# Two heads side by side in the scratch of branch outputs, and the first raw left operands loaded ahead of the last key panel

## The chip, the core and the metric

The kernel runs on one core of a Trainium2 chip. The metric is device time in microseconds. The engines are named as in the profile: PE (matrix products; PEld its weight loads), DVE (elementwise work, scans, 32x32 transposes), ACT (activations, copies; it also issues DMAs), POOL (masks, and DMAs), SP (issues DMAs only). Each engine runs its own queue in order.

## The reference

One inference step of a layer with 16 heads on 1024 prompt rows (one stream) and 128 sample rows (8 streams of 16): an input projection, eight stick-breaking heads, eight retention heads with a rotary embedding, per-head normalisation and gate, one output projection, a residual.

```python
def merge(o_sb, o_r, gate_sb, gate_r, g_sb, g_r, w_out):
    y_sb = head_rms_norm(o_sb, g_sb, gate_sb.dtype) * jax.nn.silu(gate_sb)
    y_r = head_rms_norm(o_r, g_r, gate_r.dtype) * jax.nn.silu(gate_r)
    y = jnp.concatenate([y_sb, y_r], axis=-1)
    return jnp.einsum('bte,ed->btd', y, w_out)
...
    log_beta = jax.nn.log_sigmoid(z)
    log_keep = jnp.where(strict, jax.nn.log_sigmoid(-z), 0.0)
    later = lax.cumsum(log_keep, axis=3, reverse=True) - log_keep
    a = jnp.where(strict, jnp.exp(log_beta + later), 0.0)
    return jnp.einsum('bhqk,bkhd->bqhd', a.astype(v.dtype), v)
...
    scores = jnp.einsum('bihd,bjhd->bhij', qf, kf) * intra[None]
    o = jnp.einsum('bhij,bjhe->bihe', scores, vf)
    o = o + jnp.einsum('bihd,bhde->bihe', qf, sf) * decay_read.T[None, :, :, None]
    s_new = sf * jnp.exp(lg * jnp.float32(n))[None, :, :, None] + jnp.einsum('bjhd,hj,bjhe->bhde', kf, decay_write, vf)
```

All results are float32. Each product of two float32 operands is made as three matmuls: both operands are split into a high and a low part (`wh` and `wl` for weights, `mh` and `ml` or `ah` and `al` for the other side; ACT makes the high part, DVE the low one), and high x high, high x low and low x high are added.

## The kernel before

**Stages.** Rows are worked in two groups: group 0 is row tiles 0 to 3 and the sample rows, group 1 is row tiles 4 to 7. Phase 0 does the eight heads for group 0, phase 1 for group 1. For each head of phase 1 the panels are, in order: `rows` (value and gate rows), `ret_keys` and `ret_queries` (the rotary key and query `rk` and `rq`), `attention` (stick-breaking). For the last head the order is `rows, attention, ret_keys, ret_last`: `ret_last` makes the last query panel. A panel (`project`) takes four weight loads `wr<-w_cols` (L389), each split into `wh` and `wl`, and 48 matmuls `acc` (L400).

**The output product** comes last, from about 1867 us. It is made by seven block products in Strassen's manner, numbered 1 to 7 (`n` below), each in two halves. Their left operands are branch outputs or sums of branch outputs, their right ones blocks of `w_out` or sums of them (`s_b`). A product loads its right operand in eight blocks `wr` (L1227, five buffers that it shares with the panels), splits each (L170, L171), and makes three matmuls a block and row tile (L1210, L1213, L1214). The first six halves, `FIRST`, begin while the last heads' attention and retention still finish between them.

**The scratch in between.** A finished branch output of one head (128 x rows of the group) is stored to `s_y`, one DRAM tensor a head; sums of its quarters (`sum_rows`, run by the generator `sums`, tile `br`) are stored to `s_s`, one tensor a head. `left` (L339) fetches the raw left operand of one product from there: eight heads in tiles `mr` or `yr` of two heads each, three tiles deep for `mr`, and one load a head. It issues the first three tiles, waits `wait` steps (`D_LEFT` = 18 for group 0), and then splits one head at a step into `mh` and `ml`; every second split lets the next tile be loaded. `left_sample` (L356) does the same for sample rows.

**The order of the work.** It is written by the program, not by the chip: `tick()` is called after each matmul of a panel and several times a block of a product, and each tick lets one due `Job` (a generator) emit its next step; the number it yields is how many ticks later the next step is due. `drain(job)` ticks until that job is done. `pin` holds an instruction at its place among the matmuls.

**Retention keys.** `ret_branch` needs the keys with rows and columns exchanged. It stores `rk` to `s_rk` (L648), waits `D_TO`, reads it back in four pieces into `ro` (L657: on POOL in phase 0, on SP in phase 1), waits `D_RK` (36 ticks in phase 0, 22 in phase 1), and then transposes on DVE into `rkn` (L1035), scales it (L1039), and goes on to scores `rs` (L913), outputs `pa` (L931, L936) and the state `pS` (L946). Stick-breaking weights go the same way: masks on POOL (L682), scan on DVE (L693), product `be` (L694), store `s_be` (L648), read-back (L657), transpose to `kp` (L753), and the matmuls `pa` (L790).

**The first left operand.** The product that opens the output stage, number 5 of group 0, needs its left operand `mr<-s_s` during `ret_last`: `first_left` drains the sums (`summed[0]`), and calls `left`; the panel `ret_last` is then made with its splits between the matmuls. `early_sums` are the sums of group 1's rows.

Of the kernel before, what the change touches and what calls it, by code (L numbers as in the profile page):

```python
# [21 lines left out]
H = 8  # L22
# [25 lines left out]
D_TB = (17, 24)  # L48
D_TI = (36, 13)
D_LATE = 8  # L50
D_RK = (36, 22)
D_OUT = 3
V_SET = 4
D_SUM = 6
# [4 lines left out]
D_FIN = 2  # L59
D_MR = 6  # L60
D_OP = 2
D_LEFT = 18
D_SUM2 = (4, 6, 26)
D_SUM3 = (3, 3, 6)
MR = 3
# [26 lines left out]
def tile_hybrid_step(  # L92
# [44 lines left out]
    def y_rows(t):  # L137
# [21 lines left out]
    s_v = [scr.tile([P, 4, P], F32, name=f"s_v{h}") for h in range(H)]  # L159
    s_S = [scr.tile([P, P], F32, name=f"s_S{h}") for h in range(H)]  # L160
    s_b = [[scr.tile([P, 4, 512], F32, name=f"s_b{n}_{k}") for k in range(HT)] for n in range(2)]
    s_s = [[scr.tile([P, 4, 256], F32, name=f"s_s{i}_{h}") for h in range(H)] for i in range(2)]
    s_y = [
        [scr.tile([P, g["n"]], F32, name=f"s_y{i}_{e}") for e in range(2 * H)]
        for i, g in enumerate(GROUPS)
    ]

    def split(hi, lo, src):
        return (
# [87 lines left out]
    def drain(job):  # L257
        while job is not None and not job.done:
            tick()
# [40 lines left out]
    def sum_rows(gi, h):  # L300
        def load(r):
            for kk in range(2):
                pin(nc.sync.dma_start(r[:, 2 * kk : 2 * kk + 2].rearrange("p a n -> p (a n)"), s_y[gi][kk * H + h][:, :512]))

        ops = ((3, 1, 3, "a"), (1, 0, 1, "s"), (0, 3, 0, "s"), (2, 2, 0, "s"))
        return load, ops, s_s[gi][h]

    def sums(pool, items, pace, bufs):

        def fetch(load):  # L310
            r = pool.tile([P, 4, 256], F32, name="br", tag="br", bufs=bufs)
            load(r)
            return r

        r = fetch(items[0][0])
        yield pace[2]
        for i, (_, ops, dst) in enumerate(items):
            nxt = fetch(items[i + 1][0]) if i + 1 < len(items) else None
            for o, a, b, how in ops:
                pin(nc.vector.tensor_tensor(r[:, o], r[:, a], r[:, b], ALU.add if how == "a" else ALU.subtract))  # L320
                yield pace[0]
            yield pace[1]
            pin(nc.scalar.dma_start(dst, r))
            r = nxt
            yield pace[2]

    def left(gi, n, hi, lo, bufs, tag, deep, wait):
        src = LEFT[n]
        raw = []

        def load(pair):
            r = bufs.tile([P, 2, 256], F32, name=tag, tag=tag, bufs=deep)
            for i in range(2):
                h = 2 * pair + i
                if src[0] == "y":
                    rows = s_y[gi][src[1] * H + h][:, src[2] * 256 : src[2] * 256 + 256]
                else:
                    rows = s_s[gi][h][:, src[1], :]
                pin(nc.sync.dma_start(r[:, i], rows))  # L339
                raw.append(r[:, i])  # L340

        for pair in range(deep):
            load(pair)
        yield wait
        for h in range(HT):
            pin(*split(hi[h], lo[h], raw.pop(0)))
            if h % 2 and h // 2 + deep < HT // 2:
                load(h // 2 + deep)
            yield D_OP

    def left_sample(kk, hi, lo, bufs, tag, deep, wait):
        raw = []
        for part in range(2):
            r = bufs.tile([P, HT // 2, P], F32, name=tag, tag=tag, bufs=deep)
            for i in range(HT // 2):
                pin(nc.sync.dma_start(r[:, i], s_y[0][kk * H + part * HT // 2 + i][:, 4 * P : 5 * P]))  # L356
                raw.append(r[:, i])
# [113 lines left out]
    with ExitStack() as s1:  # L471
# [332 lines left out]
        def decode(h, qs, rest):  # L804
# [99 lines left out]
                )  # L904
            out.done(0)
            oT = op.tile([P, P], F32, name="doT", tag="doT", bufs=1)
            Job(out.finish(0, 0, h, 4, oT, s_y[0][h][:, 4 * P : 5 * P]))

        def retention(gi, g, h, out, rq, rk, rkn, rv, dT):
            def scores(i, kind):  # L910
# [111 lines left out]
        def ret_branch(gi, g, h, rows_in, rk):  # L1022
            rv = values[gi, h][:, :, 1, :]
            nt = len(g["tiles"])
            rkn = ep.tile([P, 6, P], F32, name="rkn", tag="rkn")

            out = Out(nt, "ro")
            dT = op.tile([P, 2, P], F32, name="dT", tag="dT", bufs=1)
            tied(nc.sync.dma_start(dT, c_dt[:, h]))
            s = turn_out(rk[:, : nt * P].rearrange("p (k t) -> p k t", t=P), f"s_rk{gi}_{h}")  # L1030
            yield D_TO[phase[0]]
            raw = out.o.rearrange("p k d -> p (k d)")
            turn_in(s, raw, back[phase[0]])
            yield D_RK[phase[0]]
            tied(nc.vector.transpose(rkn.rearrange("p k d -> p (k d)")[:, : nt * P], raw))  # L1035
# [3 lines left out]
            nc.vector.tensor_scalar(rkn[:, :4, :], rkn[:, :4, :], dec[:, h, 1:2], None, ALU.mult)  # L1039
# [3 lines left out]
            yield from out.finish(1, gi, h, 0, rkn.rearrange("p k d -> p (k d)"), s_y[gi][H + h])  # L1043

        def sb_branch(gi, g, h, out, q2, k2, kT, rest):
            tiles, nt = g["tiles"], len(g["tiles"])
            off = 0 if gi == 0 else 4
            nc.scalar.dma_start(k_prompt[h, :, tiles[0] * P : (tiles[0] + 4) * P], kT[:, :NB_TOK])
            if SAMPLE in tiles:
                nc.scalar.dma_start(k_sample[h], kT[:, 4 * P : 5 * P])  # L1050
            if gi == 0:
                nc.scalar.dma_start(s_k[h], kT[:, :NB_TOK])
            yield D_NAT[phase[0]]
            rows = yield from stick_breaking(g, h, out, q2, k2, rest)
            store_rows(tiles, values[gi, h][:, :, 0, :], v_prompt, v_sample, h)
            if gi == 0:
                nc.scalar.dma_start(s_v[h], values[gi, h][:, :4, 0, :])
            yield from out.finish(0, gi, h, 0, rows[2][1] if gi else kT, s_y[gi][h][:, :NB_TOK])
# [5 lines left out]
        summed, sampled, mine = [], [], {}  # L1064

        def kept(i):
            return [[half[i][:, h // 2, h % 2 * 256 : h % 2 * 256 + 256] for h in range(HT)] for half in mov]
# [8 lines left out]
            return left_sample(0, *mine["s", 0], wp, "mr", MR, D_LEFT)  # L1076

        def first_left():
            drain(summed[0])
            mine[0, 5] = kept(0)  # L1080
            return left(0, 5, *mine[0, 5], wp, "mr", MR, D_LEFT)

# [2 lines left out]
        for gi, g in enumerate(GROUPS):  # L1085
# [6 lines left out]
            for h in range(H):  # L1092
# [11 lines left out]
                def ret_queries(acc=None):  # L1104
                    rows_in["rq"] = rope(acc or project(g, mov, col(4, h)), "rq", *ropes)

                def ret_keys(acc=None):
                    nonlocal ret_job
                    acc = acc or project(g, mov, col(5, h))
                    drain(ret_job)  # L1110
                    ret_job = Job(ret_branch(gi, g, h, rows_in, rope(acc, "rk", *ropes)), D_NAT[phase[0]])

                def ret_last():
                    rest = first_left()
                    next(rest)
                    ret_queries(project(g, mov, col(4, h), rest))
                    for _ in rest:
                        pass
                    drain(sampled[0])

# [177 lines left out]
    with ExitStack() as s3:  # L1298
# [112 lines left out]
        ready = [Job(left_sample(1, *mine["s", 1], fp, "ys", 2, D_LEFT // 2), 24)]  # L1411
# [195 lines left out]
```

## Time and profile before

| | |
|---|---|
| median of three runs | 2256.67 us (2253.02, 2256.67, 2259.68) |
| profiled execution | 2256.29 us |
| its span in the profile | 2254.4 us |
| mean granted clock of PE | 0.996 |
| phase 1, end of the last panel | about 1867 us after the start |
| first products (`FIRST`) | about 1867 to 1979 us |
| DMA traffic | 471.24 MB, 209 GB/s on average |

A row of the timeline gives the start, the time from the first to the last of the instructions it joins, engine, line of the kernel, operation, what is written and read, and how many; brackets hold the engine's idle time before it and what ended it. SPq rows are DMAs that SP issues: the time is that of issuing, not of the transfer. A row of the waits tells what PE stood still for: total, number of times, longest. A row of windows gives the busy time of PE, PEld, DVE, ACT and POOL, then PE's granted clock, the busy share of the 16 DMA engines and GB/s. A 128x512 matmul is listed with 0.39 us but one starts every 0.23 us, since they overlap.

### The profile page before, as it was taken

How to read it: one execution, taken by the hardware profiler on the slowest of the kernel's cores; microseconds unless marked ns; L12 is line 12 of the kernel's file. 1: busy time of each engine (PE TensorE's matmuls, PEld its weight loads, DVE VectorE, ACT ScalarE, POOL GpSimd, SP SyncE). 2: the span in 40 equal slices, each digit the busy share in tenths (PEclk: the TensorE clock that was granted, in tenths of full speed). 3: DMA queues.
4: the chain of work that ended last, by engine and by line, in shares of the span. 5: the costliest groups of instructions: out<-in, count | busy, mean ns of one | idle time of the engine just before them, and what ended most of it. 6: DMA issues, size and time to landing. Idle time of an engine off the chain costs nothing.

```text
span 2254.4 us, 34741 instructions
## 1 busy us (share of the span) xinstructions
PE 2219.5 (98%) x12002; PEld 1884.7 (84%) x12002; DVE 1266.5 (56%) x2688; ACT 922.2 (41%) x2000; POOL 434.6 (19%) x724
## 2 busy tenths in 40 slices
PE   8999999999999999999999999999999999999998
PEld 7888889798888979888788888888888887778886
DVE  5335445453554545355666665766566666556677
ACT  6423333333333333334434344343433445545563
POOL 1022131322213232221312112020302212000020
PEclk9999999999999999999999999999999999999999
DMA  8567575576656657577768887887888776865786
GB/s 295 168 198 201 176 198 176 174 195 205 190 178 188 195 173 200 186 206 266 234 187 228 241 232 236 243 229 231 232 238 230 226 210 182 226 217 162 218 217 175
DMA packets 383984, 471.24 MB, mean 209 GB/s; under 512 B 121408, under 2 KB 238656, under 8 KB 383296
## 3 DMA queue, kind: packets, MB, share of 16 engines
q1 hardware_dynamic: 253712, 290.98, 43.7%
q0 software_dynamic: 36432, 95.72, 15.2%
q10 hardware_dynamic: 93664, 82.33, 11.9%
q8 instruction: 94, 1.54, 0.3%
q14 instruction: 82, 0.67, 0.1%
HBM read 367.97 MB, written 110.36 MB: 212 GB/s over the span
## 4 chain that ended last, share of the span: by engine, by line
PE 86%; DMA 6%; DVE 3%; issue 3%; ACT 1%; POOL 0%; SPq 0%; ACTq 0%; DVEq 0%; POOLq 0%
PE accm L457 33%; PE acc L400 28%; PE a L1214 5%; PE a L1213 5%; PE a L1210 5%; PE z L763 2%; PE pa L790 2%; PE zc L831 1%; DMA wr<-w_out 1%; PE pd L892 1%; DMA xc<-x_cols 1%; PE rs L913 1%; PE pa L931 1%; PE pS L946 1%; DMA wr<-w_cols 1%
## 5 line engine op out<-in xcount | busy, mean ns | idle before, releaser
L170 ACT ACTIVATE wh<-wr 128x512 fp32r<-128x512 f32 x408 | 257.1, 631 | 486.6 <-PE acc L400 207.2
L457 PE MATMUL accm<-whn,mh 128*128 128x512 f32 x1152 | 452.6, 393 | 2.0 <-DVE rq L503 1.0
L457 PE MATMUL accm<-whn,ml 128*128 128x512 f32 x1152 | 451.9, 393 | 0.0
L457 PE MATMUL accm<-wln,mh 128*128 128x512 f32 x1152 | 451.5, 392 | 0.0
L400 PE MATMUL acc<-mh,wh 128*128 128x256 f32 (+2 forms) x1536 | 444.0, 340 | 7.5 <-ACT wh L170 7.5
L400 PE MATMUL acc<-ml,wh 128*128 128x256 f32 (+2 forms) x1536 | 445.0, 340 | 0.0
L400 PE MATMUL acc<-mh,wl 128*128 128x256 f32 (+2 forms) x1536 | 443.5, 339 | 0.0
L171 DVE TENSOR_TENSOR wl<-wr,wh 128x512 fp32r<-128x512 f32 x408 | 279.6, 688 | 281.8 <-ACT wh L170 258.2
L171 DVE TENSOR_TENSOR wln<-wrn,whn 128x512 fp32r<-128x512 f32 x256 | 175.3, 688 | 270.7 <-ACT whn L170 268.0
L170 ACT ACTIVATE whn<-wrn 128x512 fp32r<-128x512 f32 x256 | 161.2, 632 | 393.4 <-PE accm L457 258.8
L400 PEld LDWEIGHTS acc<-mh,wh 128*128 128x128 f32 x1536 | 283.8, 189 | 26.7 <-ACT wh L170 7.5
L400 PEld LDWEIGHTS acc<-mh,wl 128*128 128x128 f32 x1536 | 281.7, 188 | 24.4 <-issue 5.4
L400 PEld LDWEIGHTS acc<-ml,wh 128*128 128x128 f32 x1536 | 281.1, 189 | 19.1 <-issue 1.2
L457 PEld LDWEIGHTS accm<-whn,mh 128*128 128x128 f32 x1152 | 216.5, 188 | 47.5 <-DVE rq L503 2.1
L457 PEld LDWEIGHTS accm<-whn,ml 128*128 128x128 f32 x1152 | 216.5, 188 | 43.5 <-issue 0.8
L457 PEld LDWEIGHTS accm<-wln,mh 128*128 128x128 f32 x1152 | 216.4, 188 | 42.9
L657 POOL DMA_DIRECT2D be<-s_be x128 | 93.8, 739 | 160.6 <-DMA s_be<-be 132.9
L693 DVE TENSOR_TENSOR_SCAN kp<-kp 128x1152 f32<-128x1152 f32 (+4 forms) x40 | 82.6, 2066 | 64.5 <-POOL kp L682 36.5
L1210 PE MATMUL a<-wh,mh 128*128 128x512 f32 x240 | 95.6, 398 | 0.8 <-ACT mh L1270 0.8
L1213 PE MATMUL a<-wl,mh 128*128 128x512 f32 x240 | 94.4, 393 | 1.5 <-DVE wl L171 1.4
L1214 PE MATMUL a<-wh,ml 128*128 128x512 f32 x240 | 94.4, 393 | 0.0
L682 POOL TENSOR_SCALAR_AFFINE_SELECT kp<-kp 128x128 f32<-128x128 f32 x40 | 13.7, 342 | 374.3 <-ACT kp L676 369.2
(287 smaller groups left out, 3002.7 us busy)
## 6 DMA issues: line engine op xcount, KB each, us to landing
wr<-w_cols SPq DMA_DIRECT2D x256, 256.0 KB, 4.5
wrn<-w_rows SPq DMA_DIRECT2D x256, 256.0 KB, 3.7
kcT<-cache_k POOLq DMA_DIRECT2D x64, 512.0 KB, 5.0
vc<-cache_v SPq DMA_DIRECT2D x64, 512.0 KB, 5.4
wr<-s_b SPq DMA_DIRECT2D x80, 256.0 KB, 4.2
wr<-w_out SPq DMA_DIRECT2D x80, 256.0 KB, 4.2
br<-w_out SPq DMA_DIRECT2D x64, 256.0 KB, 4.8
s_b<-br ACTq DMA_DIRECT2D x32, 512.0 KB, 5.2
```

Source lines behind the costliest of these rows:

```text
L170: nc.scalar.activation(hi, src, AF.Copy),
L171: nc.vector.tensor_tensor(lo, src, hi.bitcast(F32), ALU.subtract),
L400: last = nc.tensor.matmul(a[:, :m], lhs[:, j, :], rhs[w][:, j, o : o + m], start=(w == 0 and j == 0 and n == 0), stop=(w == KT // WQ - 1 a ...
L457: anchor[0] = nc.tensor.matmul(banks[t], lhs[q][:, j, ts], rhs, start=(k == 0 and n == 0), stop=(k == KT - 1 and n == 2),)
L657: q.dma_start(raw[32 * i : 32 * i + 32, :].rearrange("p (k a) -> p k a", a=32), s[:, :, 32 * i : 32 * i + 32].rearrange("k (j b) a -> b (k ...
L693: nc.vector.tensor_tensor_scan(rev, rev, rev, 1.0, ALU.mult, ALU.bypass)
L763: nc.tensor.matmul(z[:, :c], q2[a][:, i * P : (i + 1) * P], k2[b][:, s : s + c], start=(m == 0), stop=(m == 2),)
L790: nc.tensor.matmul(po[:, :P], at[:, j, :], rest["vn"][j], start=(j == 0), stop=(j == t))
L831: mm = nc.tensor.matmul(z[r, :], qp[:, j, r], ks[2 * j + c // 2][0][:, c % 2, :], start=(j == 0), stop=(j == 1),)
L1210: ins = nc.tensor.matmul(a, hi[k][:, ts], wh, start=first, stop=False)
L1213: nc.tensor.matmul(a, hi[k][:, ts], wl, start=False, stop=False)
L1214: anchor[0] = nc.tensor.matmul(a, lo[k][:, ts], wh, start=False, stop=last)
```

## The change

Scratch tensors `s_s` and `s_y` now hold two heads side by side (`y_of` gives one head's part). `left` fetches a tile of two heads in one load of 128x2x256 instead of two of 128x256, and `left_sample` makes four loads of 128x2x128 instead of eight. `first_left` is called at the start of the last head's `ret_keys`, one panel earlier, so that its first three loads are issued there; it no longer drains the sums whole, but ticks until the sums of group 0's rows are stored (`stored`); `ret_last` drains the rest. `D_RK` grows from 22 to 28 ticks in phase 1, `D_LEFT` from 18 to 24; the last stage's wait goes from `D_LEFT // 2` = 9 to `D_LEFT // 3` = 8. What is computed stays.

```diff
-D_RK = (36, 22)
+D_RK = (36, 28)
-D_LEFT = 18
+D_LEFT = 24
-    s_s = [[scr.tile([P, 4, 256], F32, name=f"s_s{i}_{h}") for h in range(H)] for i in range(2)]
+    s_s = [[scr.tile([P, 2, 4, 256], F32, name=f"s_s{i}_{p}") for p in range(H // 2)] for i in range(2)]
     s_y = [
-        [scr.tile([P, g["n"]], F32, name=f"s_y{i}_{e}") for e in range(2 * H)]
+        [scr.tile([P, 2, g["n"]], F32, name=f"s_y{i}_{p}") for p in range(H)]
...
+    def y_of(gi, e):
+        return s_y[gi][e // 2][:, e % 2, :]
...
+            stored[0] += 1
...
             r = bufs.tile([P, 2, 256], F32, name=tag, tag=tag, bufs=deep)
-            for i in range(2):
-                h = 2 * pair + i
-                if src[0] == "y":
-                    rows = s_y[gi][src[1] * H + h][:, src[2] * 256 : src[2] * 256 + 256]
-                else:
-                    rows = s_s[gi][h][:, src[1], :]
-                pin(nc.sync.dma_start(r[:, i], rows))
-                raw.append(r[:, i])
+            if src[0] == "y":
+                rows = s_y[gi][src[1] * H // 2 + pair][:, :, src[2] * 256 : src[2] * 256 + 256]
+            else:
+                rows = s_s[gi][pair][:, :, src[1], :]
+            pin(nc.sync.dma_start(r, rows))
+            raw.extend((r[:, 0], r[:, 1]))
...
         def first_left():
-            drain(summed[0])
+            while stored[0] < HT + H:
+                tick()
...
                 def ret_keys(acc=None):
                     nonlocal ret_job
+                    if (gi, h) == (1, H - 1):
+                        lefts.append(first_left())
+                        next(lefts[0])
...
                 def ret_last():
-                    rest = first_left()
-                    next(rest)
-                    ret_queries(project(g, mov, col(4, h), rest))
-                    for _ in rest:
+                    drain(summed[0])
+                    ret_queries(project(g, mov, col(4, h), lefts[0]))
+                    for _ in lefts[0]:
                         pass
...
-                made.append(left(g, n, *mine[g, n], *((rp, "yr", 2) if g else (wp, "mr", MR)), D_LEFT // 2))
+                made.append(left(g, n, *mine[g, n], *((rp, "yr", 2) if g else (wp, "mr", MR)), D_LEFT // 3))
```

The order of instructions is the same through phase 0; from the middle of phase 1 it differs. Three places:

SP's queue at the end of the last head, before (`so` is the read-back of attention rows, `br` the sums of group 1, `wr<-w_cols` the last key panel, `wr<-s_b` the first product, `mr` its raw left operand, `ro<-s_rk` the key read-back):

```order
L657 DMA so<-s_o_6_4_1_18140 32x16x32 x4
L303 DMA br<-s_y_13_167 128x512
L389 DMA wr<-w_cols 128x512
L1227 DMA wr_18526<-s_b_0_106 128x512
L1227 DMA wr_18532<-s_b_1_107 128x512
L1227 DMA wr_18538<-s_b_2_108 128x512
L1227 DMA wr_18587<-s_b_3_109 128x512
L339 DMA mr<-s_s_0_122 128x256
L339 DMA mr<-s_s_1_123 128x256
L339 DMA mr<-s_s_2_124 128x256
L339 DMA mr<-s_s_3_125 128x256
L339 DMA mr<-s_s_4_126 128x256
```

The same queue with the change:

```order
L662 DMA so<-s_o_6_4_1_18113 32x16x32 x4
L343 DMA mr<-s_s_0_122 128x2x256
L343 DMA mr<-s_s_1_123 128x2x256
L343 DMA mr<-s_s_2_124 128x2x256
L306 DMA br<-s_y_2_140 128x512
L306 DMA br<-s_y_6_144 128x512
L394 DMA wr<-w_cols 128x512 x2
L1235 DMA wr_18494<-s_b_0_106 128x512
L1235 DMA wr_18500<-s_b_1_107 128x512
L1235 DMA wr_18506<-s_b_2_108 128x512
L1235 DMA wr_18547<-s_b_3_109 128x512
L1235 DMA wr_18570<-s_b_4_110 128x512
```

Three double loads stand ahead of the first four blocks of `s_b`, where six single ones stood behind them; the fourth pair now follows `s_b_4`, and two loads of the key panel and two of `br` come behind the three.

POOL's queue for the last head's attention weights, before (`s_be_6` and `s_be_7` are its last two row tiles):

```order
L648 DMA s_be_6_18659<-be 128x7x128
L657 DMA be<-s_be_6_18659 32x28x32 x4
L682 AFFINE_SELECT kp<-kp 128x128
L682 AFFINE_SELECT be<-be 128x128
L648 DMA s_be_7_18801<-be 128x8x128
```

With the change:

```order
L653 DMA s_be_6_18626<-be 128x7x128
L687 AFFINE_SELECT kp<-kp 128x128
L687 AFFINE_SELECT be<-be 128x128
L662 DMA be<-s_be_6_18626 32x28x32 x4
L653 DMA s_be_7_18785<-be 128x8x128
```

The masks of the last row tile come ahead of the read-back of the one before. On DVE, the scan of that tile before:

```order
L719 SCALAR_TENSOR_TENSOR ro<-ro,or,gg 128x128 x4
L171 TENSOR_TENSOR wl_18789<-wr_18786,wh_18788 128x512
L171 TENSOR_TENSOR wl_18818<-wr_18815,wh_18817 128x512
L793 COPY so<-pa 128x128
L171 TENSOR_TENSOR wl_18856<-wr_18853,wh_18855 128x512
L171 TENSOR_TENSOR wl_18876<-wr_18873,wh_18875 128x512
L693 SCALAR_TENSOR_TENSOR kp<-kp 128x1024
```

With the change (the block `wl_18757` is what `wl_18789` was):

```order
L956 SCALAR_TENSOR_TENSOR S<-S,pS 128x128
L698 SCALAR_TENSOR_TENSOR kp<-kp 128x1024
L945 SCALAR_TENSOR_TENSOR ro<-pa,dec,ro 128x128
L699 TENSOR_TENSOR be<-be,kp 128x1024
L956 SCALAR_TENSOR_TENSOR S<-S,pS 128x128
L190 TENSOR_SCALAR ov<-ssq_18372 128x4
L174 TENSOR_TENSOR wl_18757<-wr_18754,wh_18756 128x512
```

The scan and the product `be` have moved ahead of the norm (`ov`, then `ro`) and of four weight splits.

SP's queue at the key read-back of retention head 4 in phase 1, before (`br<-w_out` feeds the sums of weights):

```order
L657 DMA ro<-s_rk_4_15237 32x16x32
L295 DMA br<-w_out 128x2x256 x2
L657 DMA ro<-s_rk_4_15237 32x16x32 x3
L389 DMA wr<-w_cols 128x512 x2
L448 DMA wrn<-w_rows 128x512
```

With the change:

```order
L394 DMA wr<-w_cols 128x512 x3
L662 DMA ro<-s_rk_4_15213 32x16x32 x4
L298 DMA br<-w_out 128x2x256 x2
L394 DMA wr<-w_cols 128x512 x2
L453 DMA wrn<-w_rows 128x512
```

The four pieces of the read-back are no longer parted by two loads for the sums, which now follow them.

More of the change, by code (lines that the diff above doesn't have):

```diff
@@ L302, in load @@
             for kk in range(2):
-                pin(nc.sync.dma_start(r[:, 2 * kk : 2 * kk + 2].rearrange("p a n -> p (a n)"), s_y[gi][kk * H + h][:, :512]))
+                pin(nc.sync.dma_start(r[:, 2 * kk : 2 * kk + 2].rearrange("p a n -> p (a n)"), y_of(gi, kk * H + h)[:, :512]))
         ops = ((3, 1, 3, "a"), (1, 0, 1, "s"), (0, 3, 0, "s"), (2, 2, 0, "s"))
-        return load, ops, s_s[gi][h]
+        return load, ops, s_s[gi][h // 2][:, h % 2]
+    stored = [0]
     def sums(pool, items, pace, bufs):
@@ L354, in left_sample @@
             r = bufs.tile([P, HT // 2, P], F32, name=tag, tag=tag, bufs=deep)
-            for i in range(HT // 2):
-                pin(nc.sync.dma_start(r[:, i], s_y[0][kk * H + part * HT // 2 + i][:, 4 * P : 5 * P]))
-                raw.append(r[:, i])
+            for i in range(2):
+                pair = (kk * H + part * HT // 2) // 2 + i
+                pin(nc.sync.dma_start(r[:, 2 * i : 2 * i + 2], s_y[0][pair][:, :, 4 * P : 5 * P]))
+            raw.extend(r[:, i] for i in range(HT // 2))
         yield wait
@@ L906, in decode @@
             oT = op.tile([P, P], F32, name="doT", tag="doT", bufs=1)
-            Job(out.finish(0, 0, h, 4, oT, s_y[0][h][:, 4 * P : 5 * P]))
+            Job(out.finish(0, 0, h, 4, oT, y_of(0, h)[:, 4 * P : 5 * P]))
         def retention(gi, g, h, out, rq, rk, rkn, rv, dT):
@@ L1042, in ret_branch @@
             yield from retention(gi, g, h, out, rows_in["rq"], rk, rkn, rv, dT)
-            yield from out.finish(1, gi, h, 0, rkn.rearrange("p k d -> p (k d)"), s_y[gi][H + h])
+            yield from out.finish(1, gi, h, 0, rkn.rearrange("p k d -> p (k d)"), y_of(gi, H + h))
         def sb_branch(gi, g, h, out, q2, k2, kT, rest):
@@ L1057, in sb_branch @@
                 nc.scalar.dma_start(s_v[h], values[gi, h][:, :4, 0, :])
-            yield from out.finish(0, gi, h, 0, rows[2][1] if gi else kT, s_y[gi][h][:, :NB_TOK])
+            yield from out.finish(0, gi, h, 0, rows[2][1] if gi else kT, y_of(gi, h)[:, :NB_TOK])
         def from_h(k):
@@ L1062, in from_h @@
             return x_cols[:, KT * o + k * n : KT * o + (k + 1) * n]
-        summed, sampled, mine = [], [], {}
+        summed, sampled, lefts, mine = [], [], [], {}
         def kept(i):
@@ L1410, in tile_hybrid_step @@
         Job(load_gpost(), 40)
-        ready = [Job(left_sample(1, *mine["s", 1], fp, "ys", 2, D_LEFT // 2), 24)]
+        ready = [Job(left_sample(1, *mine["s", 1], fp, "ys", 2, D_LEFT // 3), 24)]
         for p in range(4):
```

## The prediction

> **What bounds the kernel now.** I read the page first (busy times, then the chain that ended last), then the waits of PE, then the windows and timelines around the longest of them.
>
> ```profile
> span 2254.4 us, 34741 instructions
> ...
> PE 2219.5 (98%) x12002; PEld 1884.7 (84%) x12002; DVE 1266.5 (56%) x2688; ACT 922.2 (41%) x2000; POOL 434.6 (19%) x724
> ...
> PE 86%; DMA 6%; DVE 3%; issue 3%; ACT 1%; POOL 0%; SPq 0%; ACTq 0%; DVEq 0%; POOLq 0%
> ```
>
> PE is busy for 2219.5 of 2254.4 us and carries 86% of the chain. The change leaves the matmuls alone, so it can give only what PE loses elsewhere: its waits, and time at a lower clock. The waits of PE (engine, what waits, for what: total, times, longest):
>
> ```profile
> PE pa L790 <- DVE kp L753: 3.9, 3, 3.5
> PE rs L913 <- DVE rq L505: 2.9, 3, 2.5
> PE a L1210 <- ACT wh L170: 1.7, 1, 1.7
> PE pS L946 <- DVE rkn L1039: 1.6, 1, 1.6
> ...
> PE a L1213 <- DVE wl L171: 1.4, 1, 1.4
> ...
> PE a L1210 <- ACT mh L1270: 0.8, 1, 0.8
> ```
>
> All six longest members fall after 1500 us, where this change moves instructions. The last columns of the following windows are the granted clock, the DMA share and GB/s.
>
> ```profile
> 1864.00:1868.00 4.00, 4.00 (x20) 3.30 (x19) 2.76 (x4) 1.13 (x3) 0.05 (x1) 1.00 1.02 313
> ...
> 1875.10:1881.90 6.80, 6.04 (x19) 5.27 (x20) 3.94 (x10) 1.20 (x4) 3.40 (x6) 0.50 0.71 186
> ...
> 1928.00:1933.00 5.00, 1.52 (x13) 1.40 (x13) 3.83 (x8) 2.82 (x7) 0.00 (x0) 1.00 0.67 222
> ...
> 1991.10:1994.60 3.50, 3.50 (x10) 2.68 (x10) 2.96 (x7) 2.62 (x7) 0.00 (x0) 0.51 0.93 315
> ...
> 1996.00:2050.00 54.00, 54.00 (x240) 44.71 (x239) 24.96 (x45) 21.64 (x48) 0.00 (x0) 1.00 0.46 143
> ```
>
> Two stretches run at half clock, 6.8 and 3.5 us long: 3.4 and 1.7 us of work lost, 5.1 together. The last row prices a matmul, and so a tick of the products: 54.00 / 240 = 0.225 us.
>
> **Part A: the first loads ahead of the last key panel.** SP's queue, then what ACT, DVE and PE waited for (the bracket: idle time before, and what ended it):
>
> ```profile
> 1845.13 11.13 SPq L1227 DMA_DIRECT2D wr<-s_b  x4
> 1856.32 3.18 SPq L339 DMA_DIRECT2D mr<-s_s  x6
> ...
> 1862.17 1.25 SPq L339 DMA_DIRECT2D mr<-s_s  x2
> ...
> 1869.40 0.77 ACT L170 ACTIVATE mh<-mr 128x256 fp32r<-128x256 f32 x2 [4.27 <-DMA mr<-s_s]
> ...
> 1875.16 0.65 DVE L505 TENSOR_TENSOR rq<-rq,sw 128x512 f32<-128x512 f32 x1
> ...
> 1872.14 0.50 PE L1213 MATMUL a<-wl,mh 128*128 128x512 f32 x1 [1.39 <-DVE wl L171]
> ...
> 1875.86 0.80 PE L913 MATMUL rs<-rq,rk 128*128 128x128 f32 x2 [2.53 <-DVE rq L505]
> ```
>
> The six raw loads stand behind four weight loads that hold SP for 11.13 us (they wait for buffers of the ring). The last pair, issued at 1862.17, lands at 1869.40, after DMA engines at share 1.02. ACT stands still for 4.27 us, and behind it on its queue are the weight split and the copies for rq; so PE waits 1.39 us for wl, then 2.53 us for rq, and the half clock begins at 1875.1. Price of the place: 1.39 + 2.53 + 3.4 = 7.3 us.
>
> In the changed order three double loads stand ahead of those four weight loads, near 1844: about 12 us earlier. The fourth still waits for the split of the first two heads, near 1861, and has one weight load more ahead of it. But the traffic beside it lacks six loads of 128 KB, 0.77 MB, which at 313 GB/s is 2.5 us. So ACT is free 2.5 us earlier at least and 4.27 at most. That ends the 1.39, and leaves of the 2.53 at most 1.4 (3.92 - 2.5). The first rs also stands one matmul later (0.225 us). Bounds of the gain: 2.5 (the lower clock stays) and 7.3; I take 1.39 + 1.7 + 3.4 = 6.5, since one short wait would remain where two stood.
>
> *Against it, the panel's weights.* Two loads of w_cols now follow the so read-back, three mr and two br on SP. Nine issues at 0.53 us (3.18 / 6 above) put them some 4.8 us later. Covered: the split that uses the first of them ran at 1851.62, its load was issued at 1839.90 and a load of this kind lands in 4.5 us (the first and last row below), so 7 us are spare before ACT, and PE comes later still. Cost 0; if that cover is gone, up to 3 us and a clock drop.
>
> ```profile
> 1839.90 0.33 SPq L389 DMA_DIRECT2D wr<-w_cols  x1
> ...
> 1851.62 1.39 ACT L170 ACTIVATE wh<-wr 128x512 fp32r<-128x512 f32 x2
> ...
> wr<-w_cols SPq DMA_DIRECT2D x256, 256.0 KB, 4.5
> ```
>
> [...]
>
> **Part C: the last attention head's weights.** The longest wait, and the chain behind it:
>
> ```profile
> 1894.75 3.01 POOL L657 DMA_DIRECT2D be<-s_be  x4 [3.42 <-DMA s_be<-be]
> 1897.76 0.75 POOL L682 TENSOR_SCALAR_AFFINE_SELECT kp<-kp 128x128 f32<-128x128 f32 x1
> ...
> 1903.10 2.29 DVE L693 TENSOR_TENSOR_SCAN kp<-kp 128x1024 f32<-128x1024 f32 x1
> ...
> 1907.24 0.90 POOL L648 DMA_DIRECT2D s_be<-be  x1 [8.04 <-DVE be L694]
> ...
> 1930.31 1.24 DVE L753 STREAM_TRANSPOSE kp<-be 128x1024 f32<-128x1024 f32 x1
> ...
> 1931.61 1.16 PE L790 MATMUL pa<-vo,kp 128*128 128x128 f32 x8 [3.48 <-DVE kp L753]
> ```
>
> Scan, product, store, read-back, transpose: 28 us from 1903.10 to PE's wait. The order now puts POOL's two selects ahead of the read-back (3.42 us of wait plus 3.01 of issue saved there), and the scan nine rows earlier on DVE, ahead of the norm of the retention rows and of four weight splits. The store can move from 1907.24 to about 1899, 8 us, against 3.48 missing. I take 3.0; bounds 0 (the read-back again lands behind weight loads) and 3.5. The price: scan and product, 2.29 + 1.22 us (1905.61 below), stand ahead of weight splits. Lower bound 0, upper 3.5; PE was busy 42.22 of 43.00 us there, and its only wait was the 0.8 of B, so I take 1.0.
>
> ```profile
> 1905.61 1.22 DVE L694 TENSOR_TENSOR be<-be,kp 128x1024 f32<-128x1024 f32 x1
> ...
> 1885.00:1928.00 43.00, 42.22 (x208) 34.59 (x206) 27.24 (x54) 23.86 (x54) 9.47 (x12) 1.00 0.78 193
> ```
>
> **Part B and D: the halved loads in the products.** B is the 0.8 us on mh L1270, where ACT had been kept by weight loads behind eight single mr loads; four fewer issues give 0 to 0.8, I take 0.4. D:
>
> ```profile
> 1971.41 3.77 SPq L356 DMA_DIRECT2D ys<-s_y  x8
> ...
> 1979.04 3.45 SPq L339 DMA_DIRECT2D mr<-s_y  x6
> ...
> 1988.95 1.91 ACT L170 ACTIVATE wh<-wr 128x512 fp32r<-128x512 f32 x3 [2.55 <-DMA wr<-w_out]
> ...
> 1989.63 0.73 PE L1210 MATMUL a<-wh,ah 128*128 128x512 f32 x2 [1.67 <-ACT wh L170]
> ```
>
> SP spends 3.77 + 3.45 us on 14 issues; seven take half, so the weight loads go out 3.6 us earlier, against 1.67 us missing and 1.7 of clock. But the bytes stay and the DMA share here is 0.93, so issues may not be what limits. Bounds 0 and 3.4; half, 1.7.
>
> **Part E: the key read-back.** In retention head 4 two loads of w_out split the read-back, the transpose came late and PE waited:
>
> ```profile
> 1530.46 1.75 SPq L295 DMA_DIRECT2D br<-w_out  x2
> ...
> 1539.50 0.71 DVE L1035 STREAM_TRANSPOSE rkn<-ro 128x512 f32<-128x512 f32 x1 [1.83 <-DMA out<-x_prompt]
> ...
> 1875.73 0.48 DVE L1039 TENSOR_SCALAR rkn<-rkn,dec 128x512 f32<-128x512 f32 x1
> ...
> 1879.44 0.64 PE L946 MATMUL pS<-vv,rkn 128*128 128x128 f32 x2
> ```
>
> Now the four pieces go together, ahead of those loads, and DVE meets the transpose 6 ticks (1.35 us) later. That takes the 1.83 us stall of DVE, and with it most of PE's 1.6: I take 1.3, bounds 0 and 1.6. The six ticks come in eight heads; what waits for them is pS. In the last head rkn was done at 1876.21 and pS ran at 1879.4, 3 us spare, and pS moves back in PE's order too: cost 0, upper bound 8 x 1.35 = 10.8. The six ticks of the first split's wait and the one tick less of the last stage are counted in A and D.
>
> **Sum.** 6.5 + 3.0 + 0.4 + 1.7 + 1.3 = 12.9 us, less 1.0 for the splits behind the scan and 0.9 for the ring of weights, which gets less lead where PE comes sooner (DMA share 0.78 to 0.93; bounds 0 and the 3.4 of D): 11.0. The profiled execution took 2256.3 us, 0.4 under the median of 2256.67; so 2245.3. Its own range: 2239.5 (all 16.6 gained, nothing paid) to 2250.
>
> **The rivals.** (1) Only A comes; the DMA engines, not the issues, hold C and D, and their waits return a few blocks later. For: shares of 0.93 and 1.02. Against: C's chain starts with an order on POOL and DVE. Time: 2256.3 less 3 to 6.5, 2250 to 2253. (2) The loads do not do what they are there for: the fourth still lands near 1869 behind weight loads, or the half clock falls at another wait. Against: 0.77 MB less traffic. Time: 2256.3 less at most the 2.5 of the lighter traffic, 2254 to 2256. (3) Slower: the six ticks reach PE at pS. For: head 4, where pS had nothing spare. Against: the 3 us in the last head. It decides where rkn has under 1.35 us to spare; at all eight heads the time is 2256.3 + 10.8 = 2267, or 2261 if A gives its 6.5. (4) Slower: the scan ahead of the splits starves PE for the whole 3.5 us and the clock falls for 3.4: 2256.3 + 6.9 = 2263, or 2257 with A.
>
> **How the numbers follow.** Forecast 0.56 (faster in nearly all of it), rival 1 0.22 (two fifths faster), rival 2 0.10, rival 3 0.06, rival 4 0.06. A difference under 0.3%, 6.8 us, can't be told from none, so faster means under 2249.9: 0.54 + 0.10 = 0.64. Slower means over 2263.4, which takes rival 3 or 4 with A failing or both together: 0.07. Within: 0.29. The range, 2239 to 2257, holds the forecast and rivals 1 and 2, 0.88 before their edges; what these leave out brings it to 8 in 10.
>
> **What would show it.** Right: PE's waits on rq L505 and kp L753 under 1 us after 1850; clock 1.00 through 1870 to 1890; the three mr loads issued before s_b_0; SP's stretch near 1971 halved. Wrong: waits on wh or wl in the last panel or after the scan, pS waits in several heads, or a new stretch at half clock.

## The result, and the profile after

The changed kernel took 2246.88 us (median of six runs, 2244.89 to 2249.89) against 2256.38 us before (six runs, 2253.02 to 2259.68): ratio 0.9958, 95% interval 0.9946 to 0.997, 9.5 us. The forecast was 2245.3 us and "faster". The profiled executions have spans of 2243.7 and 2254.4 us, 10.7 apart.

The page of the changed kernel, and what its PE waited for from 1840 us on (total, times, longest):

```profile
span 2243.7 us, 34635 instructions
...
PE 2215.9 (99%) x12002; PEld 1884.3 (84%) x12002; DVE 1266.4 (56%) x2688; ACT 921.3 (41%) x2000; POOL 432.9 (19%) x724
...
PE 90%; DMA 3%; DVE 2%; issue 2%; ACT 1%; SPq 0%; POOL 0%; DVEq 0%; ACTq 0%; POOLq 0%
```

```profile
PE a L1218 <- ACT wh L173: 1.8, 1, 1.8
PE rs L918 <- DVE rq L510: 1.2, 1, 1.2
PE a L1218 <- ACT mh L1278: 0.8, 2, 0.6
PE a L1221 <- DVE wl L174: 0.4, 1, 0.4
```

The 3.5 us on kp, the 1.4 on wl in the last panel and the 1.6 on rkn are gone; the 2.5 on rq became 1.2; the 1.7 on wh near 1980 and the 0.8 on `mh` of the product are still there. PE's share of the chain rose from 86 to 90%.

Where the time went is read from PE's landmarks in both timelines (end of the first rows panel of phase 1, up to which PE's order is the same; first product matmul; first matmul with `ah`; last matmul):

| stretch | before | after | gain |
|---|---|---|---|
| to the end of that panel | 1092.27 | 1090.73 | 1.5 |
| from there to the first product | 774.80 | 774.16 | 0.6 |
| from there to the first `ah` | 112.58 | 103.47 | 9.1 |
| from there to the last matmul | 264.75 | 265.21 | -0.5 |

The first 1.5 us are not the change's: PE's order is the same up to there, and over the fourteen profiles of this study that panel ended anywhere from 1089.9 to 1093.1, whichever edits were in. So the gain lies in the 9.1 us of the third stretch, which holds places A, B and C.

**Place A after.** SP, ACT and PE at the last panel of the changed kernel, and a window over it with its granted clock:

```profile
1839.87 1.84 SPq L343 DMA_DIRECT2D mr<-s_s  x3
...
1847.03 7.66 SPq L1235 DMA_DIRECT2D wr<-s_b  x5
1858.08 0.53 SPq L343 DMA_DIRECT2D mr<-s_s  x1
...
1863.44 0.73 ACT L173 ACTIVATE mh<-mr 128x256 fp32r<-128x256 f32 x2 [2.87 <-DMA mr<-s_s]
...
1870.95 0.49 PE L918 MATMUL rs<-rq,rk 128*128 128x128 f32 x2 [1.24 <-DVE rq L510]
...
1864.00:1885.00 21.00, 19.76 (x106) 16.67 (x105) 17.62 (x32) 11.51 (x29) 5.26 (x9) 1.00 0.63 155
```

The three double loads went out at 1839.87, ahead of the loads of `s_b` that hold SP; the fourth pair went out at 1858.08, behind five of those loads, where the last two single ones had stood behind six. ACT still waits for the fourth pair, but 2.87 us instead of 4.27 and it ends 1.5 us before PE reaches the product (1864.89). PE waits once, 1.24 us, and the clock is 1.00 throughout the window's 21 us.

**Place C after.** POOL, DVE and PE in the last head's attention:

```profile
1884.98 0.29 POOL L687 TENSOR_SCALAR_AFFINE_SELECT kp<-kp 128x128 f32<-128x128 f32 x1 [0.80 <-ACT kp L681]
...
1885.30 2.29 DVE L698 TENSOR_TENSOR_SCAN kp<-kp 128x1024 f32<-128x1024 f32 x1 [0.59 <-POOL kp L687]
...
1891.01 0.90 POOL L653 DMA_DIRECT2D s_be<-be  x1 [0.37 <-issue]
...
1917.11 1.24 DVE L758 STREAM_TRANSPOSE kp<-be 128x1024 f32<-128x1024 f32 x1
...
1918.41 1.16 PE L795 MATMUL pa<-vo,kp 128*128 128x128 f32 x8
```

The store goes at 1891.01, 16 us earlier than before, the transpose at 1917.11, 13 us earlier, and `pa` starts without a bracket: no wait.

**Place D after.** SP, ACT, PE, and the clock:

```profile
1965.43 5.56 SPq L1235 DMA_DIRECT2D wr<-w_out  x4
1971.04 2.63 SPq L343 DMA_DIRECT2D mr<-s_y  x3
...
1976.09 0.42 ACT L173 ACTIVATE mh<-mr 128x256 fp32r<-128x256 f32 x1 [4.45 <-DMA mr<-s_y]
...
1977.08 0.50 PE L1218 MATMUL a<-wh,ah 128*128 128x512 f32 x1 [1.76 <-ACT wh L173]
...
1980.00:1982.00 2.00, 2.00 (x6) 1.55 (x5) 2.00 (x6) 1.27 (x4) 0.00 (x0) 0.50 0.85 243
```

The wait kept its size and changed its cause. Before, ACT waited for a weight load; now it waits 4.45 us for a raw operand whose load stands behind four weight loads on SP, and the weight split that PE needs is behind that on ACT. The half clock is back too.

### The profile page after: what moved, and what is told of

The parts are those of the page before. It is cut to its first block, busy times and chain, and to the rows that moved or that the text cites. A ratio compares the mean times of both kernels' runs of the same rounds, so it can differ in the third digit from the quotient of the medians.

```text
span 2243.7 us, 34635 instructions
## 1 busy us (share of the span) xinstructions
PE 2215.9 (99%) x12002; PEld 1884.3 (84%) x12002; DVE 1266.4 (56%) x2688; ACT 921.3 (41%) x2000; POOL 432.9 (19%) x724
## 4 chain that ended last, share of the span: by engine, by line
PE 90%; DMA 3%; DVE 2%; issue 2%; ACT 1%; SPq 0%; POOL 0%; DVEq 0%; ACTq 0%; POOLq 0%
PE accm L462 35%; PE acc L405 31%; PE a L1218 5%; PE a L1221 5%; PE a L1222 5%; PE pa L795 2%; PE z L768 2%; PE zc L836 1%; PE pd L897 1%; DMA s_rk<-rk 1%; PE rs L918 1%; PE pa L936 1%; PE pS L951 1%; DMA ro<-s_rk 1%; PE pa L941 1%
```

## The experiments

What had to be told apart: the early place of the loads, the pairing, and the longer D_RK. The theory at the start was that of the prediction: A comes from the early loads, C and E from D_RK. Times are medians; ratios are to runs of the kernel before on the same chip (medians 2256.0 to 2256.8). A profile shows one execution, whose time can differ from the median.

**D_RK back to 22 in the changed kernel** (e1_rk22).

```diff
-D_RK = (36, 28)
+D_RK = (36, 22)
```

> The changed kernel with the key read-back's wait D_RK put back from 28 to 22 ticks; all else as changed. Theory (the longer wait alone brings POOL's masks, the scan and the key read-back of head 4 forward; the early loads are another matter): the wait of PE on kp L758 of the last head returns with 2 to 3.5 us and the wait on rkn in head 4 with 1 to 1.6 us, while the last panel's waits stay short (rq under 1.5 us, no half clock near 1870): 2250 to 2252 us. Rival (the longer wait does nothing for PE, what was gained came with the loads): 2247 us, no wait on kp over 1 us.

2250.01 us, ratio 0.9968 (0.9957 to 0.998). From 1092 us on PE waited:

```profile
PE pa L795 <- DVE kp L758: 2.4, 3, 2.0
...
PE rs L918 <- DVE rq L510: 1.4, 3, 1.0
PE a L1221 <- DVE wl L174: 0.6, 2, 0.4
```

The wait on kp is back with 2.0 us, A's are short, as expected. The time alone would not show it: the interval overlaps the changed kernel's (0.9946 to 0.997). The profiled execution took 2245.05 us, 5 below the median, with a granted clock of 0.999 (two of the six had 0.997): its trace does not hold all that the median lost. The wait on rkn in head 4 did not come back, though the read-back is parted again there (one piece, two loads of `w_out`, three pieces): so E is not settled by this run.

**first_left back in ret_last, all else as changed** (e2_late).

```diff
-                    if (gi, h) == (1, H - 1):
-                        lefts.append(first_left())
-                        next(lefts[0])
...
                     drain(summed[0])
+                    lefts.append(first_left())
+                    next(lefts[0])
                     ret_queries(project(g, mov, col(4, h), lefts[0]))
```

> The changed kernel with first_left called again in ret_last, behind the last key panel; double loads, D_RK 28 and D_LEFT 24 stay. Theory (the place of the first three loads on SP's queue is what ends the waits of the last panel): they are issued near 1855 again, ACT waits about 4 us for mr, PE about 1.4 us for wl and 2 to 2.5 us for rq, with a half-clock stretch behind: 2252 to 2254 us. Rival (half as many loads suffice, wherever they stand): 2247 to 2249 us, PE's waits there under 1.5 us together.

2246.02 us, ratio 0.995 (0.9938 to 0.9963): no slower than the changed kernel. My theory fell here, and so did the rival's reason, as SP's queue in this run shows:

```profile
1845.06 2.60 SPq L1234 DMA_DIRECT2D wr<-s_b  x2
1847.71 2.39 SPq L343 DMA_DIRECT2D mr<-s_s  x3
1854.94 1.85 SPq L1234 DMA_DIRECT2D wr<-s_b  x3
```

With D_RK 28 the loads stand ahead of the third load of `s_b` even from `ret_last`, and it is before the third, which went out at 1854.94, that SP is held. The number meant for the key transposes moves these loads as well. By the code, each tick serves one due step, so a step that is due later lets others go ahead of it; that chain was not followed further.

**The early loads alone on the kernel before** (e3_early_single): single loads, D_RK 22, D_LEFT 18; `first_left` and `next` called in `ret_keys`, as in the change.

```diff
+                    if (gi, h) == (1, H - 1):
+                        lefts.append(first_left())
+                        next(lefts[0])
```

> The kernel before with only the early first loads: scratch of one head a tensor, two single loads a tile, D_RK 22, D_LEFT 18, but first_left called at the start of the last head's ret_keys. Theory (the place is what counts): the waits of the last panel shrink to about 1 us and the half clock there goes, 5 to 7 us; waits on kp (3.5 us) and rkn (1.6 us) stay: 2249 to 2251 us. Rival (the pairing is needed): 2254 to 2257 us, since six single issues in front of the panel's weights and the last pair behind them give the time back.

2251.39 us, ratio 0.9979 (0.9968 to 0.9989). SP's queue, and a window behind the wait on kp:

```profile
1843.72 5.07 SPq L342 DMA_DIRECT2D mr<-s_s  x6
...
1849.53 7.53 SPq L1233 DMA_DIRECT2D wr<-s_b  x5
...
1924.71:1928.12 3.41, 3.41 (x15) 3.02 (x14) 1.68 (x7) 0.61 (x3) 0.00 (x0) 0.50 0.22 78
```

PE's waits on rq fell to 0.4 us at most and those on wl to 0.2; kp kept 3.1 and rkn 1.8, and here 3.4 us of half clock came behind the wait on kp, where the kernel before had none. As the theory said: alone, the early place is worth about 5 us, and no pairing is needed for it.

**D_RK 28 alone on the kernel before** (e7_b_rk28).

```diff
-D_RK = (36, 22)
+D_RK = (36, 28)
```

> The kernel before with only D_RK raised from 22 to 28 ticks in phase 1. Theory (it carries the waits on kp and rkn, and nothing of the last panel's): PE's wait on kp falls from 3.5 to under 1 us, that on rkn of head 4 goes, the waits on wl and rq and the half clock near 1875 stay: 2251 to 2253 us. Rival 1 (no effect): 2256 us. Rival 2 (six ticks more make pS wait in several heads): over 2258 us, with waits on rkn of about 1 us each.

2245.0 us, ratio 0.995 (0.9938 to 0.9962): one number gives as much as the whole change, and more than the theory's 3 to 5 us. SP, then PE's longest waits from 1092 us on:

```profile
1844.20 3.02 SPq L1227 DMA_DIRECT2D wr<-s_b  x2
1847.27 4.32 SPq L339 DMA_DIRECT2D mr<-s_s  x6
...
PE a L1210 <- ACT wh L170: 2.1, 1, 2.1
PE pa L790 <- DVE kp L753: 1.0, 3, 0.5
```

The six loads went out at 1847.27 (before: 1856.32), behind two loads of `s_b` and not four. In the last panel there is no wait on rq or wl, and none on kp is over 0.5. One wait is new: 0.8 us on rkn at `pS` of the last head (1875.73), where the prediction had counted 3 us to spare. Revised theory: D_RK does A and C both, by the order that it gives, and the early call does A a second time.

**The pairing alone on the kernel before** (e8_pair): scratch of two heads and double loads, nothing else.

```diff
+            if src[0] == "y":
+                rows = s_y[gi][src[1] * H // 2 + pair][:, :, src[2] * 256 : src[2] * 256 + 256]
+            else:
+                rows = s_s[gi][pair][:, :, src[1], :]
+            pin(nc.sync.dma_start(r, rows))
+            raw.extend((r[:, 0], r[:, 1]))
```

> The kernel before with only the pairing: scratch of two heads, double loads; first_left in ret_last, D_RK 22, D_LEFT 18, last stage 9, as before. The three first loads stand behind four loads of s_b on SP's queue. Theory (it is the place behind the four weight loads that costs, whatever number of loads): the waits on wl and rq in the last panel stay near 3 to 4 us together, the half clock behind them may, the wait on kp (3 us) and on rkn of head 4 (1.6 us) stay: 2253 to 2257 us. Rival (half as many issues free SP and ACT early enough): 2248 to 2250 us, the two waits under 1.5 us.

2255.06 us, ratio 0.9992 (0.9983 to 1.0001): no difference that can be told. SP, and PE's waits from 1840 us on:

```profile
1848.91 11.06 SPq L1234 DMA_DIRECT2D wr<-s_b  x4
1860.03 1.92 SPq L343 DMA_DIRECT2D mr<-s_s  x3
...
PE a L1220 <- DVE wl L174: 3.6, 3, 2.0
PE rs L918 <- DVE rq L510: 2.5, 1, 2.5
PE pa L795 <- DVE kp L758: 2.3, 2, 2.1
```

Behind four loads of `s_b`, three double loads are as late as six single ones.

**The loads moved into the last panel of the changed kernel** (e9_in_panel): this undoes A's place while D_RK stays 28.

```diff
                     drain(summed[0])
+                    lefts.append(first_left())
                     ret_queries(project(g, mov, col(4, h), lefts[0]))
```

The first `next` then comes after 12 of the panel's 48 matmuls.

> The changed kernel with the first left operand's loads issued inside ret_last, after the first 12 of its 48 matmuls, which puts them behind five loads of s_b; D_RK 28, D_LEFT 24 and the pairing stay. Theory (with D_RK 28 the loads are early enough already because they stand ahead of the third load of s_b; behind it SP is held and the waits return): mr loads issued after 1855, PE's waits on wl and rq near 1870 together 3 to 5 us with half clock possible, kp under 1 us: 2250 to 2254 us. Rival (D_RK 28 removes the last panel's waits in another way than by the loads' place): 2246 us, those waits under 1.5 us.

2248.22 us (2247.49 to 2249.24), ratio 0.9962 (0.9949 to 0.9975), about 2 us above e2_late's 2246.02, with intervals that overlap. The place itself is plain:

```profile
1843.86 11.73 SPq L1233 DMA_DIRECT2D wr<-s_b  x5
1855.64 1.99 SPq L343 DMA_DIRECT2D mr<-s_s  x3
...
1870.20 0.50 PE L1219 MATMUL a<-wl,mh 128*128 128x512 f32 x1 [0.72 <-DVE wl L174]
1873.68 0.79 PE L918 MATMUL rs<-rq,rk 128*128 128x128 f32 x2 [2.06 <-DVE rq L510]
...
1874.00:1876.00 2.00, 2.00 (x7) 1.61 (x7) 2.00 (x5) 0.21 (x1) 1.89 (x3) 0.50 0.21 69
```

Loads at 1855.64, waits of 2.8 us together, half clock behind them. So in the traces the place of the loads is what ends A's waits, though the two medians alone would not show it; from the first product to the first `ah` this kernel took 106.64 us against 103.35 in e2_late, 3.3 more, of which some 1.4 are the clock (2.9 us of work at half speed). That is less than the 5 us of e3_early_single: the half clock here lasted 3.4 us (0.93 on average from 1866 to 1890), in the kernel before 6.8.

**D_RK 30 and D_RK 34 on the kernel before** (e11_rk30, e12_rk34): two numbers chosen by the order that they give. In the programs as they are written for 22 to 36 (only 22, 28, 30 and 34 were run) the order does not follow the number: at 22 and 26 four loads of `s_b` stand ahead of `mr`, at 23, 28, 30 and 34 two; POOL's last two masks stand ahead of the read-back at 28 and 34, behind it at 22, 24, 25, 27, 30 and 32, and one on each side at 23, 26 and 36.

```diff
-D_RK = (36, 22)
+D_RK = (36, 30)
```

> The kernel before with D_RK 30 instead of 22 in phase 1, nothing else. With this number the six first loads stand behind two loads of s_b on SP, as with 28, but POOL's last two masks stand behind the read-back and the scan late on DVE, as with 22. Theory (D_RK acts by the order that it happens to give, not by the longer wait): PE's waits on wl and rq near 1870 under 1.5 us together, its wait on kp of the last head 2 us or more: 2248 to 2252 us, between 22 and 28. Rival (the transposes must only come late enough): at least as good as 28, 2243 to 2246 us, with kp under 1 us.

```diff
-D_RK = (36, 22)
+D_RK = (36, 34)
```

> The kernel before with D_RK 34 in phase 1, nothing else: twelve ticks more than before, and an order like that with 28 in both places (six loads behind two of s_b, masks ahead of the read-back, the scan early). Theory (the order counts): the same waits gone as with 28, 2244 to 2247 us. Rival (28 is the right length; six ticks more reach PE at pS, 8 x 1.35 us at most): over 2250 us with waits on rkn in several heads.

30: 2250.81 us, ratio 0.998 (0.9972 to 0.9989). 34: 2245.69 us, ratio 0.9956 (0.9944 to 0.9969). The intervals do not meet, and 34 stands with 28 on the far side of 30. PE's waits from 1840 us on with 30, and with 34:

```profile
PE pa L790 <- DVE kp L753: 4.5, 2, 3.6
PE rs L913 <- DVE rq L505: 1.8, 1, 1.8
PE pa L931 <- DVE sc L915: 1.3, 1, 1.3
...
PE a L1213 <- DVE wl L171: 0.2, 1, 0.2
```

```profile
PE a L1210 <- ACT wh L170: 2.1, 1, 2.1
PE pa L936 <- DVE S L951: 1.0, 1, 1.0
PE pa L790 <- DVE kp L753: 0.8, 1, 0.8
```

With 30 A is mended in part: the wait on wl and the half clock there are gone (1.00 from 1866 to 1890), but 1.8 us on rq are left, more than the theory allowed, and 1.3 on `sc` are new, with the first six loads in the same place as with 28. So the loads' place is not all that sets A; what else does was not tested. C is not mended: POOL stored `s_be_7` at 1902.37 against 1891.46 with 28, PE waited 3.6 us on kp, and half clock for 3.4 us came behind that (128x512 matmuls 0.43 us apart from 1928.96 on, 0.23 from 1930.21 on). With 34, twelve ticks more than before, A and C are both mended and PE waits on rkn nowhere. What counts is the order, not the length.

**The last stage's wait, 16 instead of 8** (e6_last16), to move two weight splits ahead of the split on which ACT stood in place D; the same number on the kernel with D_RK 28 alone (e10_rk28_last16), and on e2_late (e13_late_last16).

```diff
-                made.append(left(g, n, *mine[g, n], *((rp, "yr", 2) if g else (wp, "mr", MR)), D_LEFT // 3))
+                made.append(left(g, n, *mine[g, n], *((rp, "yr", 2) if g else (wp, "mr", MR)), 16))
...
-            ready = [Job(left_sample(1, *mine["s", 1], fp, "ys", 2, D_LEFT // 3), 24)]
+            ready = [Job(left_sample(1, *mine["s", 1], fp, "ys", 2, 16), 24)]
```

> The changed kernel with the last stage's wait of left and left_sample raised from 8 to 16 ticks, so that on ACT two more weight splits stand ahead of the first split of product 2's raw operand. Theory (what is left of the wait near 1977 comes from that split, which waits 4.45 us for its load while weight splits queue behind it on ACT): PE's wait on wh there falls from 1.8 us to under 0.5 and the half clock behind it goes, 2 to 4 us: 2243 to 2245 us. Rival (the DMA engines, at 0.95 to 1.0 there, deliver no faster): the wait stays at 1.5 to 2 us behind another load, 2247 us.

> The kernel before (single loads, first_left in ret_last, D_LEFT 18) with D_RK 28 and the last stage's wait 16 instead of 9. Theory (both numbers work by themselves and neither pairing nor early loads are needed): 2241 to 2244 us, no wait over 1 us on wh, wl, rq or kp after 1860. Rival (without the halved loads SP is the limit near 1980): the wait on wh there stays at 2 us, 2245 us.

> The changed kernel with first_left back in ret_last and the last stage's wait 16 instead of 8: pairing, D_RK 28 and D_LEFT 24 stay. Theory (early loads are not needed beside D_RK 28, and the last stage's short wait costs what is left near 1977): 2242 to 2245 us, no half clock near 1980. Rival: 2246 us, as without the 16.

e6_last16: 2245.52 us, 0.995 (0.9937 to 0.9963). e10_rk28_last16: 2243.73 us, 0.9944 (0.993 to 0.9958). e13_late_last16: 2245.62 us, 0.9955 (0.9942 to 0.9968). None can be told apart from the changed kernel's 0.9958 (0.9946 to 0.997). In the profile of e6_last16, at place D:

```profile
1980.44 0.50 PE L1221 MATMUL a<-wl,ah 128*128 128x512 f32 x1 [0.86 <-DVE wl L174]
...
1968.00:1990.00 22.00, 20.35 (x85) 15.52 (x84) 17.26 (x42) 13.86 (x33) 0.00 (x0) 1.00 0.90 298
```

The wait on wh in front of 1977 is gone and the clock is 1.00 (the changed kernel: 19.86 us busy and 0.92 in the same window), but 0.86 on wl, and two waits of 0.5 and 0.2 us by 1987, stand in their place. So ACT's queue was the cause of D in the changed kernel, as the theory had it, and the window holds five matmuls more (85 against 80), about 1.1 us; the median does not show that much clear of its interval. In e10_rk28_last16, with single loads, PE still waited 2.32 us on wh there: its time came as the theory said, its reason failed. In e13_late_last16 the half clock near 1980 went as expected (128x512 matmuls 0.23 us apart from 1981.27 on) and 0.9 on wl stood in place of the wait on wh, but 1.7 on rq came near 1871, and its time fits the rival.

**D_LEFT 18 in the changed kernel** (e5_left18).

```diff
-D_LEFT = 24
+D_LEFT = 18
```

> The changed kernel with D_LEFT 18 instead of 24, the last stage's wait kept at 8. Theory (the six ticks ahead of the first split are not needed once the loads are early): 2245 to 2248 us, waits on wl and rq near 1870 under 1.5 us together. Rival (split earlier, ACT stands in front of loads that have not landed, with weight splits behind it): ACT's wait on mr over 4 us in the last panel, 2249 to 2252 us.

2244.74 us, ratio 0.9956 (0.9942 to 0.9971): the six ticks are not needed; the waits on rq and wl are 0.4 us at most. PE waited 0.7 us on rkn in the last head.

No version is faster than the changed kernel by more than the intervals. The simplest that equals it is the kernel before with D_RK 28.

## Why the prediction was right, point by point

The time was 1.6 us from the forecast, and PE's waits fell at A and C, where the prediction saw most of the gain. Of its signs, the place of the three loads, the wait on kp and the clock from 1870 to 1890 came as written; the wait on rq stayed above its 1 us (1.24), and SP's stretch near 1971 was not halved. The rest of the working holds less well.

- **A, 6.5 us forecast.** In the changed kernel 1.39 us on wl, 1.29 of the 2.53 on rq and the 3.4 us of half clock went: 6.1 us. The size and the mechanism (loads ahead of the weight loads that hold SP) hold, shown by e3_early_single, e8_pair and e9_in_panel. Two things in it were wrong. The fourth pair does not have a weight load more ahead of it than the last pair before, but one less (five against six). And the working gives A to the early call alone and weighs D_RK only at the transposes of part E and rival 3: D_RK 28 puts the same loads ahead of the hold by itself, which the order of the changed kernel could not show, since there the early call hides it.
- **The panel's weights, 0 forecast.** Right: they went out at 1842.93 and later, and PE waited for no wh or wl in the panel.
- **C, 3.0 forecast, 1.0 paid.** 3.48 us went and nothing was paid: PE waited on no wl behind the scan. The mechanism was right, though the store moved by 16 us where 8 were forecast; that it hangs on the order that D_RK gives is shown by the waits on kp in e1_rk22, e7_b_rk28 and e11_rk30.
- **B, 0.4 forecast.** Nothing: two waits on `mh` with 0.8 us together remain.
- **D, 1.7 forecast.** Nothing, rather 0.5 lost: the wait of 1.67 became 1.76 + 0.37, and the half clock stayed. The failing step took the issues of SP as the limit and halved them with their number. The seven double loads took 2.49 + 2.63 = 5.1 us to issue where the fourteen single ones took 7.2. Four weight loads now stand ahead of the raw loads, those land later, and ACT's order turns that into the same wait.
- **E, 1.3 forecast.** The wait on rkn in head 4 went (1.58 us), but 1.00 on kp L676 appeared in that head: from its rows panel to the next head's PE took 103.24 us instead of 103.91, 0.7 gained. In e1_rk22 the wait was absent without the cause removed, so even this is not settled.
- **The ring, 0.9 paid.** None was seen.

So the sum of the parts that showed is 6.1 + 3.5 + 0.7 - 0.5 = 9.8, near the 9.5 measured, while the forecast reached 11.0 with two parts that never came and two prices that were not paid. That it came so near is in part luck: 3.2 us too much in B, D and E stand against 1.9 us of prices that nothing cost. (The range's lower end should read 2239.7, 2256.3 less 16.6; nothing hangs on it.) Of the rivals, the slower ones did not show: rkn is in no wait of the changed kernel, nor with 34 ticks; the 0.8 us with 28 alone is the most that came of rival 3.

On the clock, the forecast counted the 3.4 us of half clock in A whole, and in D half of what the wait and the half clock behind it cost (1.7 us each). In A the half clock went, in D it stayed. The length of a wait does not tell whether half clock follows: in the changed kernel A's wait of 1.24 us brought none, while 1.76 and 0.37 us in D brought 3.4 us of it, behind a window in which PE was busy for half of the time (1.73 us from 1975.77 to 1979.18); in e10_rk28_last16 a wait of 2.32 us in D brought none (granted clock of that execution 0.999). That a shorter wait would take the half clock with it was the author's estimate; what sets the half clock was not shown.

## What to carry to other kernels

In a program whose order is made by counting ticks, a number is not only a delay: it deals the order anew, and here its worth lay in two places where a queue was held. Before a gain is credited to an edit, put each edit alone on the old kernel and take each out of the new one; here two edits did the same thing, and the one that looked like a footnote gives by itself as much as all of them together. Here a load that must not be late belonged on SP's queue ahead of the weight loads that held it (11.13 us for four of them in the kernel before); behind them, three double loads were as late as six single ones (1860.03 in e8_pair, 1856.32 before).

## What the runs showed of the hardware

Half clock did not go by the length of the wait. None came after 3.48 us (before, place C) or 2.32 us (e10_rk28_last16), but 3.4 us of it after 1.76 + 0.37 us (after, place D), after 0.72 + 2.06 us (e9_in_panel), and after the waits on kp of 3.1 us (e3_early_single) and 3.6 us (e11_rk30). In the kernel before it lasted 6.8 us in A, from 1875.09 to 1881.92, and 3.4 us in D, from 1991.14 to 1994.56; there a 128x512 matmul started every 0.43 us instead of 0.23. Four windows of 3.4 us, three of the kernel before (ahead of the half clock in A, then the two that share the wait in C) and one of e11_rk30 (the wait in C):

```profile
1871.68:1875.09 3.41, 1.19 (x4) 0.67 (x4) 3.41 (x6) 3.10 (x7) 0.63 (x1) 1.00 0.63 180
...
1926.29:1929.71 3.42, 1.83 (x9) 1.17 (x7) 1.70 (x5) 2.23 (x6) 0.00 (x0) 1.00 0.98 268
1929.71:1933.12 3.41, 1.51 (x13) 1.51 (x14) 3.22 (x7) 1.85 (x5) 0.00 (x0) 1.00 0.51 167
```

```profile
1923.33:1926.74 3.41, 0.95 (x8) 0.95 (x9) 3.28 (x7) 2.39 (x7) 0.00 (x0) 1.00 0.55 191
```

PE worked 1.19 us in the first and 0.95 us in the last, and half clock came behind both; in the other two it worked 1.83 and 1.51 us, and the clock stayed at 1.00. Ahead of the half clock in D of the kernel before, PE worked 1.74 of 3.41 us (1987.73 to 1991.14), more than the 1.51 that brought none. What decides whether half clock follows, and why it lasted twice as long in A as in D, was not shown.

The first rows panel of phase 1, up to which PE's order is the same in all kernels here, ended between 1089.9 and 1093.1 us in the fourteen profiles: here a difference under 3 us between two profiled spans is not to be read as an effect.
